# A first feed-forward by seven block products, and a new order of its passes

## The chip, the cores and the metric

One core of a Trainium2 chip runs the kernel in one launch. The metric is the device time of the run in microseconds (us); smaller is better. Five engines work side by side, each through its own queue of instructions in order: TensorE (PE in the profile, with PEld for its weight loads), VectorE (DVE), ScalarE (ACT), GpSimd (POOL) and SyncE (SP, which here only issues transfers). They wait for each other by semaphores.

## The reference

Two decoder layers on x of 512 tokens by 2048 channels, float32. Each layer is a half feed-forward, a mixer, and a half feed-forward; a last norm ends it. What the change touches is the feed-forward:

```
h = h + 0.5 * swiglu(rms_norm(h, g), w_gate, w_up, w_down)
swiglu(x) = (silu(x @ w_gate) * (x @ w_up)) @ w_down
w_gate, w_up: 2048 x 1536     w_down: 1536 x 2048
```

There are four of them: (0,0) at the start, (0,1) and (1,0) between the two mixers, (1,1) at the end. The mixers (dilated attention beside latent attention; pooling beside stick-breaking attention) stay as they are.

## The kernel before

Activations are kept transposed, as 16 blocks of 128 channels by 512 tokens. Every float32 operand of a matmul is split in two: `h`, rounded by ACT to the type that PE takes (line 273 for weights, 312 or 315 for activations), and the rest `l = x - h`, by DVE (lines 274, 313, 316). A product is then three matmuls, h·h, h·l and l·h (`mm3`, lines 302 to 304).

**Weights** come in the order of a plan that is written out ahead (`plan_and_uses`). SP loads blocks of 128 x 512 into 9 `raw` buffers; `split_to` splits each into one of 7 pairs of split buffers, up to 6 blocks ahead of the block in use (`ahead`, line 284). So ACT and DVE always work on splits that PE needs some products later, and their instructions stand in their queues in the order in which the Python code emits them.

**The plain feed-forward** (`ffn`, line 473) is used for (0,0) alone: 12 gate and 12 up products over 16 blocks of channels, then 16 down products over 12 blocks. Its first 16 steps (tiles `gu`) work on two output blocks beside the loading and splitting of x; squares for the norm are summed by POOL (line 395).

**The feed-forward by products** (`ffn_products`, line 595) is used for the other three. Tokens, channels and the pair gate and up are cut in halves, and seven products of sums of blocks stand for eight (the Strassen-Winograd scheme). `Pieces` makes the sums of activations: `early` (line 559) four subtractions (line 563) and two splits per pair of channel blocks, `late` (line 575) the other three operands. The sums of weights are made in place by DVE (line 278) behind the split that used the block last. Hidden channels go in three units of 512. Per unit a pass of three products (tiles `pa`, 144 matmuls: 8 blocks k, 3 products, 2 halves of 128 tokens, 3 matmuls) and a pass of four (tiles `pb`, 192 matmuls). The four-pass needs four weight splits and four sums a k from DVE. In the order of the code: three, four of unit 0, three, four of unit 1, three, four of unit 2.

Behind each four-pass `to_hidden` (line 621) combines the results: eight additions (line 622), four Silus (lines 626, 629), four multiplications with the norm's factor (line 636), and 16 transposes on PE (line 644) per unit, whose output is split into the `hid` blocks that the down products read. It is a generator in the queue `side`; each `tick()` takes its next step. Ticks stand behind each product of the next pass of three, and behind down products for the last unit. The transposes are in PE's queue at the place where the step was emitted, and all that is emitted later waits behind them.

**Down products** (tiles `pd`): 16 output blocks; the first four (`FIRST`) run in two parts, so that units 0 and 1 can be used before unit 2 is ready. The residual comes back from DRAM (`reload`), the result goes to a sink that scales, squares and stores it.

Of the kernel before, what the change touches and what calls it, by code (L numbers as in the profile page):

```python
# [16 lines left out]
P = 128  # L17
S = 512
DM = 2048
# [35 lines left out]

FIRST = 4
# [13 lines left out]
def plan_and_uses():  # L70
# [15 lines left out]
    def ffn_products(i, j, down):  # L86


        for u in range(FF // UNIT):
            c0, c1 = u * UNIT, (u + 1) * UNIT  # L90
            block = lambda name, k: cols(name, i, j, k, k + 1, c0, c1)
            for k in range(HK):
                block("ffn_w_up", k)
                block("ffn_w_up", HK + k)
                block("ffn_w_gate", HK + k)
            for k in range(HK):
                r = len(plan)
                a22, a21, a11, a12 = r, r + 1, r + 2, r + 3
                block("ffn_w_gate", HK + k)
                block("ffn_w_gate", k)  # L100
                block("ffn_w_up", k)
                block("ffn_w_up", HK + k)
                sums[r - 3] = (a22, a21, 1, a22)
                sums[r - 2] = (a21, a11, -1, a21)
                sums[r - 1] = (a11, a22, -1, a11)
                sums[r] = (a12, a12, -1, a11)
        for n in range(0, len(down)):
            d = down[n][0]
            if n % FIRST == 0 and n < FIRST:
                for k0, k1 in ((0, 8), (8, NF)):  # L110
                    for e in down[:FIRST]:
                        cols("ffn_w_down", i, j, k0, k1, e[0] * P, e[0] * P + P)
            elif n >= FIRST:
                cols("ffn_w_down", i, j, 0, NF, d * P, d * P + P)

    def ffn(i, j, first=False):
        f = 0
        if first:
            for k0 in range(0, NK, 4):
                for ff in range(2):  # L120
                    for name in ("ffn_w_gate", "ffn_w_up"):
                        cols(name, i, j, k0, k0 + 4, ff * P, ff * P + P)
            f = 2
        for f in range(f, NF):
            for name in ("ffn_w_gate", "ffn_w_up"):
                cols(name, i, j, 0, NK, f * P, f * P + P)
        for d in range(NK):
            cols("ffn_w_down", i, j, 0, NF, d * P, d * P + P)

    ffn(0, 0, first=True)  # L130
# [86 lines left out]
def trunk(ctx: ExitStack, tc: tile.TileContext, xT, pos_row, pos_col, wts, gains, consts, bias_a_in, bias_b_in, outT):  # L217
# [131 lines left out]
    def load_x(d0, d1):  # L349
        for d in range(d0, d1):  # L350
            xs[d] = blk(f"x{d}")
            nc.sync.dma_start(xs[d], xT[d * P:(d + 1) * P, :])

    nc.scalar.dma_start(gn, gains)
    load_x(0, 4)
    load_to(2)
    load_x(4, 8)
# [78 lines left out]
    def rope_tables():  # L436
# [4 lines left out]
        for _ in range(10):  # L441
            yield
# [29 lines left out]

    def ffn(xg, norm, resid_in, sink, first=False, beside=None):
        hid = {}
        ng = norm.stages() if norm is not None else None

        def half_of(ps, name, n=HK):
            for k, wh, wl in take(name, n):
                mm3(ps, wh, wl, xg[k][0], xg[k][1], k == 0, k == NK - 1)

        def gate(ps):
            t = blk("gate")
            nc.vector.tensor_tensor(t, ps, norm.R, op=ALU.mult)
            nc.scalar.activation(t, t, AF.Silu)
            return t

        def up(f, ps, t):
            u = blk("up")
            nc.vector.tensor_tensor(u, ps, norm.R, op=ALU.mult)
            nc.vector.tensor_tensor(t, t, u, op=ALU.mult)  # L490
            hid[f] = split(t, "hid")

        f0 = 0
        if first:
            pss = [bank("gu") for _ in range(4)]
            for i in range(NK):
                half_of(pss[i % 4], ("ffn_w_gate", "ffn_w_up")[i % 2], 4)
                beside(i)
            f0 = 2
        for f in range(f0, NF):  # L500
            pg, pu = bank("pg"), bank("pu")
            half_of(pg, "ffn_w_gate")
            tick()
            if first and f == 2:
                next(ng)
            half_of(pg, "ffn_w_gate")
            if f == 0:
                next(ng)
            tick()
            half_of(pu, "ffn_w_up")  # L510
            if f == f0:
                finish(ng)
            if first and f == 2:
                up(0, pss[1], gate(pss[0]))
            t = gate(pg)
            tick()
            half_of(pu, "ffn_w_up")
            up(f, pu, t)
            if first and f == 2:
                e = gate(pss[2])  # L520
            elif first and f == 3:
                up(1, pss[3], e)
            tick()
        for job in DOWN:
            pd = bank("pd")
            for n in (8, 4):
                down_half(pd, job, hid, n)
                tick()
            down_done(pd, job, resid_in, sink)
# [65 lines left out]
    def ffn_products(pieces, norm, resid_in, sink, down):  # L595
# [25 lines left out]
        def to_hidden(u, c11, u2, s4, s5, s7, c12):  # L621
            add = lambda o, a, b: nc.vector.tensor_tensor(o, a, b, op=ALU.add)
            for a in both:
                add(s7[a], s7[a], u2[a])
                add(s4[a], s4[a], s7[a])
                nc.scalar.activation(s4[a], s4[a], AF.Silu, scale=norm.r[:, a:a + 1])
                yield
                add(s7[a], s7[a], s5[a])
                nc.scalar.activation(s7[a], s7[a], AF.Silu, scale=norm.r[:, 2 + a:3 + a])
                add(c12[a], c12[a], s5[a])  # L630
                yield
            u2.clear()
            s5.clear()
            for a in both:
                for o, g, r in ((c11, s4, a), (c12, s7, 2 + a)):
                    nc.vector.scalar_tensor_tensor(o[a], o[a], norm.r[:, r:r + 1], g[a], op0=ALU.mult, op1=ALU.mult)
                yield
            s4.clear()
            s7.clear()
            rows = c11 + c12  # L640
# [7 lines left out]
        for u in range(FF // UNIT):  # L648
            p1, p2, p4 = ([bank("pa") for _ in both] for _ in range(3))
            last = HK - 1  # L650
            for k in range(HK):
                product("ffn_w_up", "B11", p1, k, u)
                if k == last:
                    s1 = copied(p1)
                if u == 0:
                    for e in range(k + 1, min(k + 4, HK)):
                        pieces.get(e, "B11", False)
                else:
                    tick()
                product("ffn_w_up", "B21", p2, k, u)  # L660
                if k == last:
                    c11 = added(p2, s1)
                if u == 0:
                    next(late, None)
                else:
                    tick()
                product("ffn_w_gate", "T4", p4, k, u)
                if k == last:
                    s4 = copied(p4)
                if u:  # L670
                    tick()
                elif k > HK // 2:
                    next(ng, None)
            if u == 0:
                finish(ng)
                finish(late)
            del p1, p2, p4
            p5, p7, p6, p3 = ([bank("pb") for _ in both] for _ in range(4))
            for k in range(HK):
                product("ffn_w_gate", "T1", p5, k, u)  # L680
                if k == last:
                    s5 = copied(p5)
# [3 lines left out]
                if k == last:  # L686
                    s7 = copied(p7)
                if k % 2:
                    tick()
                product("ffn_w_up", "T2", p6, k, u)  # L690
                if k == last:
                    u2 = added(p6, s1, s1)
# [3 lines left out]
                if k % 2:  # L696
                    tick()
            side.append(to_hidden(u, c11, u2, s4, s5, s7, added(p3, u2)))
            del p5, p7, p6, p3, s1, c11, u2, s4, s5, s7
        pds = [bank("pd") for _ in range(FIRST)]  # L700
        for pd, job in zip(pds, down):
            for n in (4, 4):
                down_half(pd, job, hid, n)
                tick(2)
        while side:
            tick()
# [226 lines left out]
    norm = Norm(DM)  # L933
    xg = {}
    split_to(0)

    def split_x(d):
        xg[d] = split(xs[d], "xg", scale=g_norm(0)(d))

    def beside(i):  # L940
        if i in (0, 3):
            load_x(8 if i == 0 else 12, 12 if i == 0 else 16)
        if i + 4 < NK:
            split_x(i + 4)
        norm.add(xs[i])

    for d in range(4):
        split_x(d)
    u_diag, u_all = ur[:, 0:P], ur[:, P:2 * P]
    norm1, xg1 = Norm(DM), {}  # L950
    spill0 = dram_x("spill0")

    def started(i):
        beside(i)
        if i == NK - 1:
            nc.scalar.activation(ur, cs[:, 2 * P:4 * P], AF.Copy)

    side.append(rope_tables())
    ffn(xg, norm, lambda d: xs[d], make_sink(g_norm(1), norm1, xg1, spill0), first=True, beside=started)
    xs.clear()  # L960
# [262 lines left out]
```

## Time and profile before

| | us |
|---|---|
| median of 3 runs (2327.45 to 2329.95) | 2327.6 |
| the profiled execution | 2328.22 |
| its span, first to last instruction | 2326.4 |
| PE busy in it | 2249.4 |
| DVE busy | 1450.0 |
| ACT busy | 1051.5 |
| POOL busy | 185.7 |

Matmuls are pipelined: one lasts 0.39 us in the profile, but the next starts 0.23 us after it, so the time of a stretch is the number of its matmuls by the time from start to start, plus what PE waits. The mean granted TensorE clock of the execution was 0.984 of full speed. A row of a window table covers a stretch from A to B in us from the span's start; the count in brackets is that of the instructions that touch it.

### The profile page before, as it was taken

Reading aid. Unit: us, or ns where it says so; the run is one execution under the profiler, and the core shown is the slowest. Engines: PE = TensorE matmul, PEld = TensorE weight load, DVE = VectorE, ACT = ScalarE, POOL = GpSimd, SP = SyncE. Lnnn points to the kernel's source line nnn. Section 1 sums busy time; section 2 is a strip of 40 time slices with the busy share of each in tenths; the row PEclk is TensorE's granted clock in tenths of the full one; section 3 lists DMA queues with packets and bytes.
Section 4 is the critical chain, followed back from the end, with each engine's and each line's share of the span. In section 5 each row is a group of like instructions: output and inputs, shape, how many; then the busy total and the mean of one; then the engine's idle time right before and its main releaser. Section 6 shows DMA issues by size and latency. Waiting matters only on the chain.

```text
span 2326.4 us, 30133 instructions
## 1 busy us (share of the span) xinstructions
PE 2249.4 (97%) x10364; PEld 1882.2 (81%) x10364; DVE 1450.0 (62%) x2460; ACT 1051.5 (45%) x1875; POOL 185.7 (8%) x191
## 2 busy tenths in 40 slices
PE   8999999999999999889999898999999999898997
PEld 6888888989888888778788787788888888687787
DVE  5453344464645688878557787755345679788634
ACT  5332333333334575445446454433235576454443
POOL 3000011000001011000011000011200011000013
PEclk9999999999999999999999999999999999999999
DMA  6333343423224486556676565554332486565544
GB/s 219 100 87 105 104 127 114 122 64 104 74 73 124 134 250 185 166 153 185 179 192 182 165 189 152 156 181 151 98 96 69 127 238 200 154 181 164 148 140 142
DMA packets 193290, 336.94 MB, mean 145 GB/s; under 512 B 21488, under 2 KB 44400, under 8 KB 193136
## 3 DMA queue, kind: packets, MB, share of 16 engines
q1 hardware_dynamic: 163184, 280.89, 40.9%
q10 hardware_dynamic: 23904, 43.11, 5.7%
q0 software_dynamic: 6048, 11.01, 2.9%
q8 instruction: 81, 1.33, 0.2%
q14 instruction: 73, 0.60, 0.1%
HBM read 298.75 MB, written 25.17 MB: 139 GB/s over the span
## 4 chain that ended last, share of the span: by engine, by line
PE 87%; DVE 5%; issue 3%; ACT 2%; DMA 2%; POOL 0%; DVEq 0%; ACTq 0%; POOLq 0%
PE pd L303 7%; PE pd L304 7%; PE pd L302 7%; PE pb L302 5%; PE pb L304 5%; PE pb L303 5%; PE pj L302 4%; PE pj L304 4%; PE pj L303 4%; PE pa L302 3%; PE pa L303 3%; PE pa L304 3%; PE wo L302 3%; PE wo L304 3%; PE wo L303 3%
## 5 line engine op out<-in xcount | busy, mean ns | idle before, releaser
L274 DVE TENSOR_TENSOR wl<-raw,wh 128x512 fp32r<-128x512 f32 (+3 forms) x1087 | 737.2, 688 | 605.1 <-ACT wh L273 569.2
L273 ACT ACTIVATE wh<-raw 128x512 fp32r<-128x512 f32 (+3 forms) x1087 | 652.5, 609 | 749.5 <-DVE wl L274 126.3
L302 PE MATMUL pd<-hidh,wh 128*128 128x512 f32 (+1 forms) x816 | 307.9, 377 | 0.0
L304 PE MATMUL pd<-hidh,wl 128*128 128x512 f32 (+1 forms) x816 | 307.3, 377 | 0.0
L303 PE MATMUL pd<-hidl,wh 128*128 128x512 f32 (+1 forms) x816 | 307.3, 377 | 0.0
L278 DVE TENSOR_TENSOR raw<-raw,raw 128x512 f32<-128x512 f32 x288 | 196.6, 683 | 0.0
L302 PE MATMUL pj<-xgh,wh 128*128 128x512 f32 x464 | 181.7, 392 | 0.0
L304 PE MATMUL pj<-xgh,wl 128*128 128x512 f32 x464 | 180.8, 390 | 0.0
L303 PE MATMUL pj<-xgl,wh 128*128 128x512 f32 x464 | 180.7, 389 | 0.0
L302 PEld LDWEIGHTS pd<-hidh,wh 128*128 128x128 f32 x816 | 153.6, 188 | 28.1
L303 PEld LDWEIGHTS pd<-hidl,wh 128*128 128x128 f32 x816 | 153.6, 188 | 28.0
L304 PEld LDWEIGHTS pd<-hidh,wl 128*128 128x128 f32 x816 | 153.6, 188 | 27.8
L302 PE MATMUL pa<-wh,pbh 128*128 128x512 f32 x432 | 175.1, 405 | 0.0
L395 POOL TENSOR_TENSOR sq<-sq,sq 128x512 f32<-128x512 f32 (+1 forms) x65 | 81.5, 1253 | 1155.8 <-ACT sq L387 1155.8
L303 PE MATMUL pa<-wl,pbh 128*128 128x512 f32 x432 | 171.6, 397 | 0.0
L304 PE MATMUL pa<-wh,pbl 128*128 128x512 f32 x432 | 171.3, 397 | 0.0
L302 PE MATMUL pb<-wh,pth 128*128 128x512 f32 x288 | 112.2, 390 | 0.9 <-DVE s L618 0.9
L304 PE MATMUL pb<-wh,ptl 128*128 128x512 f32 x288 | 112.0, 389 | 0.0
L303 PE MATMUL pb<-wl,pth 128*128 128x512 f32 x288 | 112.0, 389 | 0.0
L304 PEld LDWEIGHTS pj<-xgh,wl 128*128 128x128 f32 x464 | 87.1, 188 | 18.2
L303 PEld LDWEIGHTS pj<-xgl,wh 128*128 128x128 f32 x464 | 87.2, 188 | 17.4
L302 PEld LDWEIGHTS pj<-xgh,wh 128*128 128x128 f32 x464 | 87.2, 188 | 17.3
(265 smaller groups left out, 3941.6 us busy)
## 6 DMA issues: line engine op xcount, KB each, us to landing
raw<-wts SPq DMA_DIRECT2D x940, 256.0 KB, 2.8
spill<-x ACTq DMA_DIRECT2D x80, 256.0 KB, 3.0
x<-spill ACTq DMA_DIRECT2D x80, 256.0 KB, 3.1
raw<-wts SPq DMA_DIRECT2D x83, 192.0 KB, 2.4
sq<-sq POOLq DMA_DIRECT2D x42, 256.0 KB, 4.9
raw<-wts SPq DMA_DIRECT2D x48, 128.0 KB, 2.4
x<-xT SPq DMA_DIRECT2D x16, 256.0 KB, 5.0
outT<-sc SPq DMA_DIRECT2D x16, 256.0 KB, 2.3
```

The costliest lines, as they stand in the source:

```text
L273: nc.scalar.activation(h, src, AF.Copy)
L274: nc.vector.tensor_tensor(low, src, f32(h), op=ALU.subtract)
L278: nc.vector.tensor_tensor(to, a, b, op=ALU.add if sign > 0 else ALU.subtract)
L302: nc.tensor.matmul(out, ah, bh, start=start, stop=False)
L303: nc.tensor.matmul(out, ah, bl, start=False, stop=False)
L304: nc.tensor.matmul(out, al, bh, start=False, stop=stop)
L395: nc.gpsimd.tensor_tensor(acc, acc, sq, op=ALU.add)
```

## The change

- Feed-forward (0,0) goes through `ffn_products` too, with its own generator `first_pieces` that makes the pieces from x beside the first pass; the plain `ffn` is gone. x is loaded in pairs between the first weight blocks; squares are summed by transfers that add (`by_dma`) and the residual is read again from `xT`.
- `PASSES` sets the order of the passes for all four: three of unit 0, three of 1, four of 0, three of 2, four of 1, four of 2. The late pieces and the norm move from the first pass into the second. Results of a pass of three are kept (`part`) until its four.
- `to_hidden` has a second `yield` behind each step of additions; a pass of four has 8 ticks instead of 16.
- The first four down products run in three parts, one per unit; `rope_tables` joins `side` only behind the second.

```diff
+PASSES = ((0, 0), (1, 0), (0, 1), (2, 0), (1, 1), (2, 1))
...
-        for u in range(FF // UNIT):
+        for u, four in PASSES:
...
-                for k0, k1 in ((0, 8), (8, NF)):
+                for k0, k1 in ((0, 4), (4, 8), (8, NF)):
...
-    ffn(0, 0, first=True)
+    ffn_products(0, 0, PAIR_DOWN)
...
-    def load_x(d0, d1):
-        for d in range(d0, d1):
+    nc.scalar.dma_start(gn, gains)
+    for k in range(HK):
+        for d in (k, HK + k):
             xs[d] = blk(f"x{d}")
             nc.sync.dma_start(xs[d], xT[d * P:(d + 1) * P, :])
-
-    nc.scalar.dma_start(gn, gains)
-    load_x(0, 4)
-    load_to(2)
-    load_x(4, 8)
+        load_to(min(3 * k + 2, NRAW - 1))
...
-        for _ in range(10):
+        for _ in range(4):
             yield
...
                 nc.scalar.activation(s4[a], s4[a], AF.Silu, scale=norm.r[:, a:a + 1])
                 yield
+                yield
                 add(s7[a], s7[a], s5[a])
                 nc.scalar.activation(s7[a], s7[a], AF.Silu, scale=norm.r[:, 2 + a:3 + a])
                 add(c12[a], c12[a], s5[a])
+                yield
                 yield
...
                     nc.vector.scalar_tensor_tensor(o[a], o[a], norm.r[:, r:r + 1], g[a], op0=ALU.mult, op1=ALU.mult)
                 yield
+                yield
             s4.clear()
             s7.clear()
+            yield
...
+        def ahead_pieces():
+            for k in range(HK):
+                for e in range(k + 1, min(k + 4, HK)):
+                    pieces.get(e, "B11", False)
+                yield
+                yield
+                yield
+
+        def then_late():
+            for _ in range(HK):
+                next(late, None)
+                yield
+                yield
+            yield from ng
...
+        def four(u):
             p5, p7, p6, p3 = ([bank("pb") for _ in both] for _ in range(4))
+            q = part.pop(u)
...
+            q["c12"] = added(p3, q["u2"])
+            turned[u] = to_hidden(u, **q)
+            side.append(turned[u])
+
+        feed = ahead_pieces() if feed is None else feed
+        rest = then_late()
+        for u, is_four in PASSES:
+            if is_four:
+                four(u)
+            elif u == 0:
+                three(u, lambda: next(feed, None))
+                finish(feed)
+            elif u == 1:
+                three(u, lambda: next(rest, None))
+                finish(rest)
+            else:
+                three(u, tick)
+                finish(turned[0])
         pds = [bank("pd") for _ in range(FIRST)]
-        for pd, job in zip(pds, down):
-            for n in (4, 4):
-                down_half(pd, job, hid, n)
+        for u in range(2):
+            finish(turned[u])
+            for pd, job in zip(pds, down):
+                down_half(pd, job, hid, UNIT // P)
                 tick(2)
-        while side:
-            tick()
+        side.extend(beside)
+        finish(turned[2])
...
+    norm0, in0 = Norm(DM, bc=False, sums=2, by_dma=True), Pieces(0)
...
+    def first_pieces():
+        for k in range(HK):
+            bs = []
+            for d in (k, HK + k):
+                b = blk("xb")
+                nc.scalar.activation(b, xs[d], AF.Copy, scale=g_norm(0)(d))
+                bs.append(b)
+            in0.add(k, *bs)
+            del bs, b
+            next(in0.work[k])
+            yield
+            finish(in0.work[k])
+            yield
+            for d in (k, HK + k):
+                norm0.add(xs.pop(d))
+            yield
+        nc.scalar.activation(ur, cs[:, 2 * P:4 * P], AF.Copy)
+
+    feed = first_pieces()
+    split_to(0)
+    for _ in range(5):
+        next(feed)
+    ffn_products(in0, norm0, reload([xT[d * P:(d + 1) * P, :] for d in range(NK)], PAIRS),
+                 make_sink(g_norm(1), norm1, xg1, spill0), PAIR_DOWN, feed, [rope_tables()])
```

In `three(u, beside)`, `beside()` stands behind each of the 24 products of the pass; the products themselves are as before.

## Rows read from the trace of the kernel before

**Rows 1.** The page's part 1: busy us, share of the span, instructions.
```profile
PE 2249.4 (97%) x10364; PEld 1882.2 (81%) x10364; DVE 1450.0 (62%) x2460; ACT 1051.5 (45%) x1875; POOL 185.7 (8%) x191
```

**Rows 2.** Windows by stage: stretch, length, busy by engine, granted clock, DMA share, GB/s.
```profile
0.00:57.03 57.03, 48.72 (x192) 38.93 (x193) 29.71 (x42) 33.49 (x57) 19.80 (x19) 0.97 0.65 219
...
276.05:406.61 130.56, 130.56 (x578) 108.11 (x576) 63.19 (x80) 47.16 (x79) 18.13 (x14) 1.00 0.38 121
...
841.51:1233.31 391.80, 373.10 (x1650) 306.84 (x1648) 283.43 (x466) 196.26 (x333) 20.52 (x16) 0.97 0.64 179
1233.31:1622.65 389.34, 372.38 (x1650) 306.47 (x1648) 281.68 (x431) 186.15 (x315) 27.57 (x17) 0.98 0.58 169
1915.81:2314.39 398.58, 378.00 (x1812) 316.86 (x1810) 274.21 (x442) 196.96 (x348) 33.70 (x26) 0.97 0.56 162
```

**Rows 3.** The list of waits of PE: us in total, times, longest.
```profile
PE ht L644 <- DVE s L636: 53.4, 21, 7.3
```

**Rows 4.** Windows by pass of feed-forward (1,0): three, four, three, first down products.
```profile
1311.31:1355.73 44.42, 36.96 (x161) 29.70 (x160) 33.03 (x53) 20.89 (x35) 0.00 (x0) 0.92 0.51 143
1355.73:1399.25 43.52, 43.52 (x193) 36.05 (x192) 37.34 (x60) 22.81 (x38) 0.00 (x0) 1.00 0.68 194
1399.25:1444.03 44.78, 37.37 (x162) 30.12 (x160) 33.12 (x53) 21.02 (x35) 0.00 (x0) 0.89 0.50 142
...
1487.55:1505.58 18.03, 15.94 (x78) 12.77 (x76) 14.74 (x24) 6.86 (x12) 0.00 (x0) 1.00 0.40 100
```

**Rows 5.** The chain that ended last: start, length, what.
```profile
1115.61 0.87 PE ht L644 x8
1257.95 1.68 PE nps L402 x16
```

**Rows 6.** Timeline of DVE, second three-pass of (1,0): start, length, instruction, idle before.
```profile
1314.28 1.41 DVE L622 TENSOR_TENSOR s<-s,s 128x512 f32<-128x512 f32 x2
...
1317.67 1.29 DVE L622 TENSOR_TENSOR s<-s,s 128x512 f32<-128x512 f32 x2
...
1320.28 1.41 DVE L622 TENSOR_TENSOR s<-s,s 128x512 f32<-128x512 f32 x2
...
1328.13 1.41 DVE L636 SCALAR_TENSOR_TENSOR s<-s,r,s 128x512 f32<-128x512 f32 x2
```

**Rows 7.** Timeline of ACT in the same stretch.
```profile
1315.79 0.72 ACT L626 ACTIVATE s<-s,r 128x512 f32<-128x512 f32 x1 [3.64 <-DVE s L622]
1316.41 0.62 ACT L273 ACTIVATE wh<-raw 128x512 fp32r<-128x512 f32 x1
```

**Rows 8.** Timeline of PE in the same stretch: the first transpose.
```profile
1327.01 0.48 PE L644 MATMUL ht<-cs,s 128*128 128x128 f32 x1 [6.01 <-DVE s L636]
```

**Rows 9.** Timeline of DVE in a pass of four.
```profile
1275.23 0.68 DVE L274 TENSOR_TENSOR wl<-raw,wh 128x512 fp32r<-128x512 f32 x1
1275.83 0.69 DVE L278 TENSOR_TENSOR raw<-raw,raw 128x512 f32<-128x512 f32 x1
```

**Rows 10.** Timeline of PE at the start.
```profile
5.90 0.79 PE L302 MATMUL gu<-xgh,wh 128*128 128x512 f32 x1 [5.90 <-ACT xgh L315]
...
24.90 0.50 PE L303 MATMUL gu<-xgl,wh 128*128 128x512 f32 x1 [2.41 <-DVE xgl L316]
```

**Rows 11.** Windows of 4 us at the start.
```profile
8.00:12.00 4.00, 4.00 (x11) 3.22 (x11) 2.34 (x4) 1.55 (x3) 0.00 (x0) 1.00 1.06 400
...
24.00:28.00 4.00, 3.10 (x8) 2.46 (x9) 3.46 (x5) 1.76 (x3) 0.96 (x2) 0.67 0.76 255
```

**Rows 12.** Timeline of ACT at the start.
```profile
18.23 0.71 ACT L315 ACTIVATE xgh<-x,gn 128x512 fp32r<-128x512 f32 x1
...
19.88 0.71 ACT L315 ACTIVATE xgh<-x,gn 128x512 fp32r<-128x512 f32 x1
```

**Rows 13.** Timeline of DVE while a piece is made.
```profile
801.76 0.42 DVE L563 TENSOR_TENSOR t<-xb 128x256 f32<-128x256 f32 x1
...
803.23 0.68 DVE L899 TENSOR_TENSOR x<-wo,x 128x512 f32<-128x512 f32 x1
```

More of the change, by code (lines that the diff above doesn't have):

```diff
@@ L86, in ffn_products @@
     def ffn_products(i, j, down):
-        for u in range(FF // UNIT):
+        for u, four in PASSES:
             c0, c1 = u * UNIT, (u + 1) * UNIT
             block = lambda name, k: cols(name, i, j, k, k + 1, c0, c1)
-            for k in range(HK):
+            for k in range(HK if not four else 0):
                 block("ffn_w_up", k)
@@ L95, in ffn_products @@
                 block("ffn_w_gate", HK + k)
-            for k in range(HK):
+            for k in range(HK if four else 0):
                 r = len(plan)
@@ L114, in ffn_products @@
                 cols("ffn_w_down", i, j, 0, NF, d * P, d * P + P)
[L116 to L128, printed above, removed]
-    ffn(0, 0, first=True)
+    ffn_products(0, 0, PAIR_DOWN)
     for half in range(2):
@@ L470, in rope_tables @@
         rope_b["cos"], rope_b["sin"] = cb, sb
[L473 to L502, printed above, removed]
-            tick()
[L504 to L526, printed above, removed]
-                down_half(pd, job, hid, n)
-                tick()
-            down_done(pd, job, resid_in, sink)
     def down_half(pd, job, hid, n):
@@ L593, in get, with ffn_products @@
             return self.of[k].pop(name) if last else self.of[k][name]
-    def ffn_products(pieces, norm, resid_in, sink, down):
+    def ffn_products(pieces, norm, resid_in, sink, down, feed=None, beside=()):
         hid = {}
@@ L646, in to_hidden, with three @@
                 hid[u * (UNIT // P) + f] = split(pt, "hid")
-        for u in range(FF // UNIT):
+        def ahead_pieces():
[11 more added lines that the diff above has]
+            yield from ng
+        last = HK - 1
+        part, turned = {}, {}
+        def three(u, beside):
             p1, p2, p4 = ([bank("pa") for _ in both] for _ in range(3))
-            last = HK - 1
+            q = part[u] = {}
             for k in range(HK):
@@ L653, in ffn_products @@
                 if k == last:
[L654 to L659, printed above, removed]
+                    q["s1"] = copied(p1)
+                beside()
                 product("ffn_w_up", "B21", p2, k, u)
                 if k == last:
[L662 to L666, printed above, removed]
+                    q["c11"] = added(p2, q["s1"])
+                beside()
                 product("ffn_w_gate", "T4", p4, k, u)
                 if k == last:
[L669 to L677, printed above, removed]
+                    q["s4"] = copied(p4)
+                beside()
+        def four(u):
             p5, p7, p6, p3 = ([bank("pb") for _ in both] for _ in range(4))
+            q = part.pop(u)
+            s1 = q.pop("s1")
             for k in range(HK):
@@ L681, in ffn_products @@
                 if k == last:
-                    s5 = copied(p5)
+                    q["s5"] = copied(p5)
                 if k % 2:
@@ L686, in ffn_products @@
                 if k == last:
-                    s7 = copied(p7)
-                if k % 2:
-                    tick()
+                    q["s7"] = copied(p7)
                 product("ffn_w_up", "T2", p6, k, u)
                 if k == last:
-                    u2 = added(p6, s1, s1)
+                    q["u2"] = added(p6, s1, s1)
                 if k % 2:
@@ L695, in ffn_products @@
                 product("ffn_w_up", "B22", p3, k, u)
[L696 to L699, printed above, removed]
+            q["c12"] = added(p3, q["u2"])
[15 more added lines that the diff above has]
+                finish(turned[0])
         pds = [bank("pd") for _ in range(FIRST)]
-        for pd, job in zip(pds, down):
-            for n in (4, 4):
-                down_half(pd, job, hid, n)
+        for u in range(2):
+            finish(turned[u])
+            for pd, job in zip(pds, down):
+                down_half(pd, job, hid, UNIT // P)
                 tick(2)
-        while side:
-            tick()
+        side.extend(beside)
+        finish(turned[2])
         for pd, job in zip(pds, down):
@@ L930, in pe_rope @@
         nc.gpsimd.tensor_tensor(v, a, b, op=ALU.add)
[L933 to L949, printed above, removed]
+    norm0, in0 = Norm(DM, bc=False, sums=2, by_dma=True), Pieces(0)
     norm1, xg1 = Norm(DM), {}
     spill0 = dram_x("spill0")
[L953 to L960, printed above, removed]
+    u_diag, u_all = ur[:, 0:P], ur[:, P:2 * P]
+    def first_pieces():
[21 more added lines that the diff above has]
+                 make_sink(g_norm(1), norm1, xg1, spill0), PAIR_DOWN, feed, [rope_tables()])
     xg, norm = xg1, norm1
```

## The prediction

> **What bounds the kernel now.** I read the page's busy shares first: PE is busy 97% of 2326.4 us [rows 1], so only fewer matmuls or fewer idle stretches of TensorE can shorten the run. Then one table of windows by stage [rows 2]. The down products of the first feed-forward are the plain case: 576 matmuls in 130.56 us, 0.2267 us from start to start (p below), no idle time. The first feed-forward ends at 406.61 us; its first 57.03 us hold only 192 matmuls, whose pace would be 43.5. The three feed-forwards that are products already take 391.80 and 389.34 us, and the last 398.58 with the output. Their floor is 7 products x 8 k x 2 halves x 3 units x 3 = 1008 matmuls (228.5), 48 transposes at 0.87/8 (5.2), 16 matmuls of the norm (1.68) [rows 5] and the down products (130.56): 366.0. So the first two lose 25.8 and 23.4 us; the last I take at their mean, 24.6, because its passes have the same code. Together 73.8.
>
> Where that lies: the list of waits has one entry of weight for PE, the transposes of line 644 waiting for the products of line 636 on DVE, 53.4 us in 21 waits [rows 3]. The table by pass [rows 4] shows it: a pass of four products takes 43.52 us, exactly 192p, and loses nothing; the pass of three after it takes 44.42 and 44.78 where 144p + 16 transposes are 34.4; the first stretch of down products takes 18.03 where 60p + 16 transposes are 15.3. The granted clock of these three-passes is 0.89 to 0.92: after the long wait part of the matmuls run at the lower level. So 10 + 10 + 3 us a feed-forward.
>
> Why it waits, from the timeline [rows 6 to 8]. The pass of three starts at 1311.31. `to_hidden` emits an addition step at every tick, one per product. A step is two additions on DVE, then Silu on ACT; the next weight split on ACT stands behind that Silu in order, DVE's half of the split behind that, and the next additions behind that. So steps start at 1314.28, 1317.67, 1320.28: 3.4 us after a step of the first kind, 2.6 after the second, while PE goes on 1.36 us (6p) per product. PE reaches the first transposes after 42 matmuls, 9.5 us into the pass, and waits 6.01 us at once; the last product of line 636 starts at 1328.13 and a pair takes 1.41, 18.2 us into the pass.
>
> **The change, part by part.** Durations are of the profiled execution (2328.2 us with what lies around its span; median of the runs 2327.6), and the sum is made against it.
>
> (a) The half pace. Idle yields now stand between the steps, and the transposes come at the 14th tick instead of the 7th. In the third pass of three (the pass after `four(0)`) PE meets them after 14 products, 84p = 19.0 us. On DVE the first step still starts 3.0 us in; between steps there is one more split (0.60 from one DVE instruction to the next [rows 9]), so steps follow at 4.0, 3.2, 4.0, 3.2, and then two pairs of line 636 (1.41 each) with two splits between (1.2): 3.0 + 14.4 + 1.4 + 1.2 + 1.4 = 21.4. PE waits 21.4 - 19.0 = 2.4 us; I take 2.3, since the first three transposes need not wait for the last product. In its place of 10. What the wait leaves behind is late splits: DVE enters `four(1)` some 4 us behind its usual lead, and makes it good there, since a four-pass costs it 32 x 1.2 = 38.6 of 43.5 us.
>
> (b) The order three, three, four, three, four, four. The second pass of three has no `to_hidden` at all now, only the late pieces and the norm: its wait of 10 us goes. What is late next is `four(2)`, which carries four addition steps of unit 1 in its own eight ticks. DVE there: 25 splits with their sums at 1.2 = 30, the last additions of `four(1)` 1.3, three steps before the last split, each with the turn over ACT, 2.7 + 2.0 + 2.7: 38.7, about 39.7 us into the pass; PE needs that split 31 products in, at 42.2. It holds by 2.5 us. If it did not, PE would wait split by split: rival D. The bound from the other side is a stall of nothing.
>
> (c) The first down products. They run by unit: four products for unit 0, then unit 1's transposes in one burst, four for unit 1, then unit 2's. Unit 1's last two products on DVE end about 11.2 us into the stretch, PE arrives at 48p = 10.9: 0.3. The four splits of the turned block then stand behind one addition step of unit 2 on DVE (1.3) and a weight split that waits for ACT (1.3): PE has its second matmul 1.8 us late. Unit 2: DVE ends 25.8 us in, PE arrives at 25.4; 0.5 with the splits. So 2.1 + 0.5, in place of 3. From both sides: 0 if DVE keeps its lead, and 10, the present wait of a three-pass, if the burst meets a late DVE as it does now.
>
> (a) to (c) leave 2.3 + 2.1 + 0.5 = 4.9 us a feed-forward (bounds 0 and 12). Gains: 25.8, 23.4 and 24.6 less 4.9 each: 59.1.
>
> (d) The first feed-forward as products. Against 1728 matmuls it has 1008 + 576 = 1584, 144p = 32.6 us fewer, and 48 transposes and 8 norm matmuls more (6.0). Weights are cut 72 blocks more often (56 blocks a unit against 32), and 96 sums on DVE come in; both lie beside PE, as in the other three, where the four-pass at 43.52 shows them covered. If that cover went, DVE's 38.6 us a pass would still not set the end.
>
> Its first pass is another matter. x has to be loaded, scaled, subtracted and split beside the matmuls. By DMA: 16 blocks of x and 24 of weights in the pass, 10.5 MB; at the 400 GB/s that the start shows [rows 11] 26 us: no bound. By ACT, per k two scaled copies, two splits, two squares, three weight splits: nine instructions. Three of the same kinds take 19.88 - 18.23 = 1.65 us [rows 12], so 4.95; and the piece's splits wait for four subtractions on DVE, 803.23 - 801.76 = 1.47 us [rows 13], of which a weight split covers half: 5.7 us a k, where PE needs 18p = 4.1. ACT sets this pass. Its order: PE's first matmul now starts at 5.90 [rows 10]; here a second block of x, a second scaled copy and the subtractions come first, some 3 us more: 9. But ACT then has the first squares and the whole second piece (5 us, to 14) and six weight splits at 0.55 in its queue before anything else, and PE's second product needs the first of those: PE really starts at 15. The splits end at 17.3; the third piece takes ACT one more turn of 5.7, so PE reaches k = 2 at 23.0. Five more turns to k = 7 (51.5) and its own 4.1 end the pass at 55.6. Bounds: 51 (ACT at 4.95 without the wait) and 77 (rival C). I take 55.6; the present start, same number of blocks of x, ends at 57.03.
>
> After it: two passes of three 65.3, norm 1.7, three of four 130.6, transposes 5.2, down products 130.6, waits 4.9: ends at 393.9 against 406.61. Gain 12.7. `rope_tables` moves from the gate products into the last twelve down products: 24 ticks for some 14 steps, DVE busy there under half of the time [rows 2]; nothing. The residual is read again from xT on ACT's queue, three blocks ahead, as the other stages do; nothing, unless those loads come late, and then the wait would stand at line 539.
>
> (e) Down weights in three parts rather than two: the same blocks in another order; nothing.
>
> Sum: 59.1 + 12.7 = 71.8; 2328.2 - 71.8 = 2256.4, less 0.6 for the median: **2256 us**.
>
> **Rivals.**
> B, the half pace spreads the waits without removing them. For it: the chain DVE, ACT, ACT, DVE of [rows 6, 7] is untouched, and at 4.0 and 3.2 us for two products it is slower than PE (2.7). Against: 7 more products of room. Price: 12 us left a feed-forward, 7.1 more in each of four: 2284.
> C, the first pass at the lower clock. For it: after the idle 2.41 us at 24.90 [rows 10] the stretch 24 to 28 was granted 0.67, part of it at 1.2 GHz [rows 11]; ACT will make PE wait about 1.6 us at every k. Against: idle 1.6 is shorter than 2.41. Price: a k costs 36p = 8.2 us instead of 5.7, so the pass ends near 77: 2277. The Trainium skill, "TensorE: Matmul & The Clock Gate", section "HAM oscillation — how this bites in real kernels", speaks for this rival: where each tile's compute is short against the wait for its operand, the array is throttled again at every tile. By that rule the time would be this rival's; the trace agrees with it for the one wait of 2.41 us and shows no run of shorter ones.
> D, slower: the two passes of four in a row exhaust DVE's lead. Seven split buffers are 9.5 us of PE, less the block in use and 1.3 us of splitting 6.8. If the lag passes that (I have 4), PE waits at each split in `four(2)`, falls to 1.2 GHz, and the pass takes 384p = 87 instead of 43.5 in all four stages: 2256 + 174 = 2430. Against it: the 2.5 us in hand under (b).
> E, the gain is not there: what leaves the three-passes returns in (c) in full and the first feed-forward pays for its start what the 26.6 us of fewer instructions give: 2328.
>
> **How the numbers follow.** Forecast 0.60, own range 2238 to 2275 (waits of 1 to 9 us a feed-forward, the first pass 51 to 60). B 0.22, C 0.08, D 0.07, E 0.03. The range 2236 to 2290 leaves out D, E, the upper third of B and the thin ends. Within 0.2% (4.7 us, about what cannot be told from no change) only E: 0.03. Faster 0.90, slower 0.07.
>
> **What would show it.** In the table by pass: the second pass of three at about 34.4 us; the third at 36.6; all three of four at 43.5; the first down stretch with 96 matmuls and 32 transposes near 27.9. The waits: line 644 behind 636 under 20 us for four feed-forwards, not 53.4. The first pass of the first feed-forward ending at 51 to 60 us with PE waiting for pieces, not for DMA. Wrong would be: `pb` matmuls that wait for a weight split (D), a granted clock near 0.5 over the first 55 us (C), transposes that wait 5 us or more (B).

## The result, and the profile after

The changed kernel takes 2268.27 us (median of 4 runs, 2267.64 to 2269.59) against 2327.57 (median of 4 runs): ratio 0.9744, 95% interval 0.9727 to 0.976. Forecast were 2256 us and a range of 2236 to 2290. The profiled execution took 2269.59 us with a span of 2267.8, so 58.6 us of span are gone where 71.8 were forecast.

The page's part 1 [rows 1]: PE's share of the span went from 97 to 98%, and DVE has 120 us more to do.

```profile
PE 2218.3 (98%) x10272; PEld 1853.0 (82%) x10272; DVE 1570.6 (69%) x2694; ACT 1111.5 (49%) x2002; POOL 159.0 (7%) x190
```

The table of windows, columns as in [rows 2], first by stage (the feed-forwards (0,0), (0,1), (1,0), (1,1)), then by pass of (0,0) (three, three, four, three, two of four together, first down products), then the third pass of three in the other stages:

```profile
0.00:398.47 398.47, 377.27 (x1649) 306.85 (x1649) 311.63 (x513) 214.22 (x373) 31.99 (x33) 1.00 0.65 192
833.42:1208.66 375.24, 370.35 (x1649) 304.70 (x1648) 281.99 (x466) 194.35 (x333) 14.13 (x16) 1.00 0.66 187
1208.66:1581.38 372.72, 368.49 (x1650) 303.81 (x1648) 279.80 (x431) 184.04 (x315) 21.23 (x17) 1.00 0.60 177
1874.57:2255.83 381.26, 374.50 (x1811) 314.27 (x1809) 272.65 (x442) 194.51 (x348) 27.35 (x26) 1.00 0.58 169
...
0.00:55.62 55.62, 39.55 (x144) 28.95 (x145) 40.48 (x80) 44.46 (x80) 11.60 (x17) 1.00 0.99 298
55.62:90.11 34.49, 34.49 (x162) 28.81 (x160) 29.81 (x54) 24.56 (x48) 2.28 (x2) 1.00 0.77 223
90.11:133.63 43.52, 43.52 (x194) 36.04 (x192) 37.34 (x60) 22.80 (x38) 0.00 (x0) 1.00 0.69 194
133.63:172.99 39.36, 36.88 (x162) 29.66 (x160) 32.22 (x53) 21.53 (x36) 0.00 (x0) 0.96 0.55 161
172.99:260.31 87.32, 87.32 (x386) 72.00 (x384) 81.77 (x132) 43.72 (x74) 0.00 (x0) 1.00 0.65 182
260.31:289.43 29.12, 26.48 (x129) 21.22 (x128) 22.63 (x36) 12.65 (x24) 0.00 (x0) 1.00 0.43 125
...
944.07:983.12 39.05, 36.80 (x161) 29.44 (x160) 32.15 (x53) 21.41 (x36) 0.00 (x0) 0.96 0.56 163
1319.31:1355.84 36.53, 34.98 (x161) 28.54 (x160) 31.78 (x53) 20.25 (x35) 0.00 (x0) 1.00 0.60 174
1985.22:2024.22 39.00, 36.75 (x161) 29.44 (x160) 32.15 (x53) 21.41 (x36) 0.00 (x0) 0.96 0.55 164
```

Beside [rows 2] the four stages are 8.1, 16.6, 16.6 and 17.3 us shorter: 58.6, the whole difference of the spans. The forecast had 12.7, 20.9, 18.5 and 19.7. By pass, against [rows 4]: the second pass of three is at its matmuls' pace (34.49), two passes of four in a row take 87.32 = 2 x 43.66, and the third pass of three takes 36.53 in (1,0), as worked out, but 39.36, 39.05 and 39.00 in the others, at a granted clock of 0.96, which means that part of it ran at the lower of TensorE's two levels (1.2 and 2.4 GHz).

The longest entries of PE's list of waits (total, times, longest), against [rows 3]; line 575 is the old 644:

```profile
PE ht L575 <- DVE s L565: 14.7, 18, 2.2
PE pa L290 <- ACT pbh L300: 13.1, 5, 8.9
PE pd L290 <- ACT hidh L300: 2.9, 4, 0.7
PE pa L290 <- ACT wh L261: 2.9, 1, 2.9
```

The 53.4 us of the transposes are 14.7. Timelines of PE, then of DVE in the third pass of three of (1,0) (against [rows 6]), then of ACT in that of (0,0) (against [rows 7]):

```profile
8.90 0.80 PE L290 MATMUL pa<-wh,pbh 128*128 128x512 f32 x1 [8.90 <-ACT pbh L300]
...
14.70 0.80 PE L290 MATMUL pa<-wh,pbh 128*128 128x512 f32 x1 [2.87 <-ACT wh L261]
...
24.63 0.39 PE L290 MATMUL pa<-wh,pbh 128*128 128x512 f32 x1
...
33.69 0.50 PE L290 MATMUL pa<-wh,pbh 128*128 128x512 f32 x1 [0.74 <-ACT pbh L300]
...
51.11 0.50 PE L290 MATMUL pa<-wh,pbh 128*128 128x512 f32 x1 [1.15 <-ACT pbh L300]
...
272.59 0.44 PE L575 MATMUL ht<-cs,s 128*128 128x128 f32 x2 [1.13 <-DVE s L565]
...
275.61 0.50 PE L290 MATMUL pd<-hidh,wh 128*128 128x512 f32 x1 [0.72 <-ACT hidh L300]
...
1339.95 0.44 PE L575 MATMUL ht<-cs,s 128*128 128x128 f32 x2 [1.33 <-DVE s L565]
```

```profile
1322.28 1.41 DVE L549 TENSOR_TENSOR s<-s,s 128x512 f32<-128x512 f32 x2
1325.06 1.29 DVE L262 TENSOR_TENSOR wl<-raw,wh 128x512 fp32r<-128x512 f32 x2 [1.37 <-ACT wh L261]
1326.27 1.28 DVE L549 TENSOR_TENSOR s<-s,s 128x512 f32<-128x512 f32 x2
...
1329.48 1.41 DVE L549 TENSOR_TENSOR s<-s,s 128x512 f32<-128x512 f32 x2
...
1333.41 1.29 DVE L549 TENSOR_TENSOR s<-s,s 128x512 f32<-128x512 f32 x2
...
1339.15 1.41 DVE L565 SCALAR_TENSOR_TENSOR s<-s,r,s 128x512 f32<-128x512 f32 x2
```

```profile
138.08 1.28 ACT L553 ACT_TABLE_LOAD   x1 [3.62 <-DVE s L549]
139.38 0.72 ACT L553 ACTIVATE s<-s,r 128x512 f32<-128x512 f32 x1
```

In (1,0) the steps start 4.0, 3.2 and 3.9 us after one another, the last pair of products ends at 1340.56, 21.25 us into the pass, and PE waits 1.33 us. In (0,0) the first Silu has a load of 1.28 us ahead of it (ACT_TABLE_LOAD, by which ACT changes its table of functions). In (0,0) no Silu has run before it; in (0,1) and (1,1), which have such a load too, functions of the mixers with loads of their own came in between. The load stands in the chain DVE, ACT, ACT, DVE, so what follows in that chain comes later: PE reaches the first transposes 0.36 us later than in (1,0) and then waits 2.20 us in place of 1.33.

### The profile page after: what moved, and what is told of

The parts are those of the page before. It is cut to its first block, busy times and chain, and to the rows that moved or that the text cites. A ratio compares the mean times of both kernels' runs of the same rounds, so it can differ in the third digit from the quotient of the medians.

```text
span 2267.8 us, 30596 instructions
## 1 busy us (share of the span) xinstructions
PE 2218.3 (98%) x10272; PEld 1853.0 (82%) x10272; DVE 1570.6 (69%) x2694; ACT 1111.5 (49%) x2002; POOL 159.0 (7%) x190
## 4 chain that ended last, share of the span: by engine, by line
PE 92%; DVE 3%; ACT 1%; issue 1%; DMA 0%; POOL 0%; DVEq 0%; ACTq 0%; POOLq 0%
PE pb L291 8%; PE pb L290 8%; PE pb L292 8%; PE pd L291 7%; PE pd L292 7%; PE pd L290 7%; PE pa L290 5%; PE pa L292 5%; PE pa L291 5%; PE pj L290 5%; PE pj L292 5%; PE pj L291 5%; PE wo L290 3%; PE wo L292 3%; PE wo L291 3%; PE pr L290 2%
## 5 line engine op out<-in xcount | busy, mean ns | idle before, releaser
L262 DVE TENSOR_TENSOR wl<-raw,wh 128x512 fp32r<-128x512 f32 (+3 forms) x1159 | 780.3, 686 | 465.2 <-ACT wh L261 442.4
L266 DVE TENSOR_TENSOR raw<-raw,raw 128x512 f32<-128x512 f32 x384 | 262.4, 683 | 0.0
L290 PE MATMUL pa<-wh,pbh 128*128 128x512 f32 x576 | 230.0, 399 | 16.0 <-ACT pbh L300 13.1
L291 PE MATMUL pa<-wl,pbh 128*128 128x512 f32 x576 | 227.6, 395 | 0.3
L292 PE MATMUL pa<-wh,pbl 128*128 128x512 f32 x576 | 227.5, 395 | 0.0
L292 PE MATMUL pb<-wh,ptl 128*128 128x512 f32 x384 | 149.4, 389 | 0.0
L291 PE MATMUL pb<-wl,pth 128*128 128x512 f32 x384 | 149.4, 389 | 0.0
L290 PEld LDWEIGHTS pa<-wh,pbh 128*128 128x128 f32 x576 | 110.2, 191 | 40.2 <-ACT pbh L300 14.8
L292 PEld LDWEIGHTS pa<-wh,pbl 128*128 128x128 f32 x576 | 109.8, 191 | 25.0 <-DVE pbl L301 1.9
L291 PEld LDWEIGHTS pa<-wl,pbh 128*128 128x128 f32 x576 | 109.9, 191 | 24.1 <-DVE wl L262 2.0
```

The lines of the kernel that those rows point to most:

```text
L262: nc.vector.tensor_tensor(low, src, f32(h), op=ALU.subtract)
L266: nc.vector.tensor_tensor(to, a, b, op=ALU.add if sign > 0 else ALU.subtract)
L290: nc.tensor.matmul(out, ah, bh, start=start, stop=False)
L291: nc.tensor.matmul(out, ah, bl, start=False, stop=False)
L292: nc.tensor.matmul(out, al, bh, start=False, stop=stop)
```

## The experiments

Ratios are to the kernel before, run on the same chip (2328.5 to 2329.4 us). "After" is the changed kernel.

### The pace alone

The kernel before with nothing but the idle yields:

```diff
                 nc.scalar.activation(s4[a], s4[a], AF.Silu, scale=norm.r[:, a:a + 1])
                 yield
+                yield
...
                 add(c12[a], c12[a], s5[a])
+                yield
                 yield
...
                 yield
+                yield
             s4.clear()
             s7.clear()
+            yield
```

> The kernel before with nothing but the idle yields in to_hidden (the half pace); old order, plain first feed-forward. Theory P (the additions' chain over VectorE and ScalarE against the tick at which the transposes stand in TensorE's queue): the second and third pass of three of each feed-forward by products fall from 44.4 to 46.4 us to 36.4 to 39.4, the first down stretch loses its 2.7 us of waiting; about 18 us a stage, 2273 us in all. Rival O (the order of the passes does it, the pace only spreads the wait): under a third of that comes, 2310 us or more.

Measured: 2273.29 us, ratio 0.976 (0.9747 to 0.9774), as expected: 55 of the 59 us. Its windows: a pass of three of (1,0), the one with a table load in (0,1):

```profile
1294.22:1330.73 36.51, 34.96 (x161) 28.53 (x160) 31.77 (x53) 20.24 (x35) 0.00 (x0) 1.00 0.56 173
920.97:960.36 39.39, 36.91 (x162) 29.68 (x160) 32.13 (x53) 21.25 (x36) 0.00 (x0) 0.96 0.52 161
```

So the pace brings a waiting pass of three to 36.5 us (39.4 with a table load) in the old order too, and both such passes of a stage gain. The order isn't needed for it.

### The pace of unit 0 taken back

After, with `if u:` ahead of each new yield, so that unit 0's steps come at every product again.

> The changed kernel with the additions of unit 0 alone back at full pace (those that run in the third pass of three); units 1 and 2 and the order stay. Theory P: that pass goes from 36.4 to 39.4 us back to 44.5 to 46.5 in all four stages, about 7 us each, 2296 us. Rival O: the pass of three without additions ahead of it gives VectorE the room, the time stays at 2268 us.

Measured: 2299.29 us, ratio 0.9873 (0.986 to 0.9886), where 2296 was expected. The window of the third pass of three of (0,0), and the wait:

```profile
133.43:179.99 46.56, 37.82 (x162) 30.41 (x160) 33.11 (x53) 22.29 (x36) 0.00 (x0) 0.89 0.45 137
```

```profile
PE ht L579 <- DVE s L567: 40.1, 20, 7.3
```

31 us come back in four passes, and the granted clock of 0.89 is again that of [rows 4].

### The old order, at half the pace

The three later feed-forwards in the order three, four, three, four, three, four, the late pieces and the norm in the first pass again (by a generator of their own, which is not shown here):

```diff
+OLD = ((0, 0), (0, 1), (1, 0), (1, 1), (2, 0), (2, 1))
...
-        for u, four in PASSES:
+        for u, four in (PASSES if (i, j) == (0, 0) else OLD):
...
```

> The changed kernel with the later three feed-forwards in the old order three, four, three, four, three, four at the half pace; the first stays in the new order. Theory P: both later passes of three wait as the one of the new order does (4.5 us where ScalarE loads its Silu table, 2.0 where it has it), but the burst of unit 1's transposes in the down products goes, worth 2.7: 2261 us, slightly faster. Rival O: the order is what took the waits away, 8 us a stage come back, 2292 us.

Measured: 2264.63 us, ratio 0.9724 (0.9711 to 0.9737), where 2261 was expected. Feed-forward (1,0) and its first stretch of down products (96 matmuls, 16 transposes):

```profile
1205.55:1576.00 370.45, 367.41 (x1650) 303.76 (x1649) 279.14 (x431) 184.57 (x315) 27.56 (x17) 1.00 0.59 178
1443.57:1467.05 23.48, 23.48 (x113) 19.58 (x112) 15.96 (x26) 8.58 (x15) 0.00 (x0) 1.00 0.37 113
```

The new order is no gain at this pace. The old one has two passes of three that wait, 36.5 where 34.4 is their pace, so its second one loses some 2.1 us; but its first down products don't wait at all: 23.48 is 96p and 16 transposes. The new order has one pass that waits and a late burst of transposes among the down products: 29.12 where 96p and 32 transposes are 25.2, a loss of 3.9. So the three later stages are 1.2 to 2.3 us shorter in the old order (370.45 against 372.72 for (1,0)).

The run of the pace alone has the plain first feed-forward, and its later three stages agree with those of this run within 0.3 us. So the difference of the medians, 8.7 us, is about what the products are worth in the first feed-forward. Part by part, then, the pace brought about 55 us, the products 9, and the order took some 4 back.

### The table loaded early

After, with one Silu of a few values at the start of the first pass of four, where ACT has time:

```diff
+            if u == 0:
+                nc.scalar.activation(small("tb"), norm.r, AF.Silu)
```

> The changed kernel with one Silu of four columns on ScalarE at the start of the first pass of four, its result unused, so that the table of 1.28 us is loaded there and not in the chain of additions. Theory T (the load is in the chain and its 1.3 us also drop TensorE's clock): the third pass of three of the first, second and fourth feed-forward falls from 39.4 to 36.4 us as in the third, 2260 us. Rival: something else than the table sets those stages apart, 2268 us.

Measured: 2261.11 us, ratio 0.9709 (0.9696 to 0.9723). The third pass of three of (0,0):

```profile
133.48:169.92 36.44, 34.94 (x161) 28.53 (x160) 31.76 (x53) 20.24 (x35) 0.00 (x0) 1.00 0.56 174
```

All four stages now have 36.4 to 36.5, at a clock of 1.00. The load of 1.28 us cost 2.5 to 2.9 us a pass: 0.36 ahead of the transposes, 0.9 as their wait (2.20 in place of 1.33), and the rest as matmuls behind it at the lower clock, 0.43 us from start to start in place of 0.23.

### Silu one tick behind its additions

After, with the idle `yield` ahead of each Silu instead of behind it, so that ACT's weight splits stand ahead of a Silu that would wait for DVE. The last addition of a step now stands ahead of that `yield`, so DVE's own order stays as it was and only the Silus move:

```diff
                 add(s4[a], s4[a], s7[a])
+                yield
                 nc.scalar.activation(s4[a], s4[a], AF.Silu, scale=norm.r[:, a:a + 1])
                 yield
-                yield
                 add(s7[a], s7[a], s5[a])
+                add(c12[a], c12[a], s5[a])
+                yield
                 nc.scalar.activation(s7[a], s7[a], AF.Silu, scale=norm.r[:, 2 + a:3 + a])
-                add(c12[a], c12[a], s5[a])
-                yield
                 yield
```

> The changed kernel with each Silu one tick behind its additions, in the yield that was idle (and the last addition of the step ahead of that Silu), so that no weight split on ScalarE stands behind a Silu that waits for VectorE. Theory P says that the turn VectorE, ScalarE, ScalarE, VectorE sets the step (4.0 and 3.2 us); without it a step costs VectorE 2.5 us, under two products of TensorE (2.7), the additions end about 18 us into the third pass of three, ahead of the transposes at 19.0, and that pass is 34.6 us in all four stages, its table load included; the bursts in the down products lose about 1 us each: 2250 us. Rival V (VectorE's plain amount of work sets the end): no change, 2268 us.

Measured: 2240.18 us, ratio 0.9619 (0.9606 to 0.9633), 10 us better than expected. Windows: third pass of three of (0,0) and of (1,0), the whole of (1,0), first down products of (0,0); then what is left of the wait; then DVE's last pair of products in the third pass of three of (1,0):

```profile
133.56:168.94 35.38, 34.95 (x161) 28.53 (x160) 31.77 (x53) 21.75 (x36) 0.00 (x0) 1.00 0.61 179
1303.51:1338.05 34.54, 34.54 (x162) 28.60 (x160) 32.05 (x53) 20.49 (x35) 0.00 (x0) 1.00 0.60 184
1192.86:1559.53 366.67, 366.67 (x1650) 304.05 (x1648) 279.94 (x431) 185.85 (x315) 21.21 (x17) 1.00 0.60 180
...
255.98:281.38 25.40, 25.40 (x130) 21.33 (x128) 20.72 (x34) 10.72 (x19) 0.00 (x0) 1.00 0.37 110
```

```profile
PE ht L575 <- DVE s L565: 1.3, 6, 0.2
```

```profile
1320.94 1.41 DVE L565 SCALAR_TENSOR_TENSOR s<-s,r,s 128x512 f32<-128x512 f32 x2
```

The turn over the two engines was the cause of nearly all of the transposes' wait (14.7 us became 1.3), those of the down products too: 29.12 became 25.40, where the expectation had taken off 1 us only. The turn is shorter and not gone: the steps now start 3.4 and 2.6 us after one another, where 2.5 was expected, and the last pair of products ends 18.84 us into the pass, only 0.2 us before PE comes to the transposes at 19.04. What is left of the wait stands in the three stages with a table load. Feed-forward (1,0) takes 366.67 us, within 0.7 of the floor of 366.0, with PE busy all the time.

### The squares of x in the second pass

To shorten ACT's turn in the first pass, the squares of x go from `first_pieces` to the second pass of three, where the norm's matmuls then come five products later:

```diff
-            for d in (k, HK + k):
-                norm0.add(xs.pop(d))
...
+                if xs:
+                    norm.add(xs.pop(n // 2 + n % 2 * HK))
...
```

> The changed kernel with the 16 squares of x for the first norm on ScalarE in the second pass of three instead of the first. Theory A (ScalarE's nine instructions a k set the first pass): seven instructions, 1.04 us a k less, the pass ends at about 49 us instead of 55.6, 2262 us. Rival D (loads of x and weights set it): unchanged, 2268 us.

Measured: 2281.22 us, ratio 0.9796 (0.9782 to 0.9809): a miss. The windows of the first and the second pass, and PE's timeline of the norm:

```profile
0.00:50.75 50.75, 38.84 (x145) 28.20 (x146) 39.84 (x81) 37.40 (x66) 0.20 (x4) 0.97 0.78 271
50.75:104.24 53.49, 41.00 (x162) 32.44 (x160) 32.95 (x56) 31.56 (x62) 13.60 (x15) 0.81 0.83 202
```

```profile
92.14 0.59 PE L387 MATMUL nps<-ones,sq 128*128 128x1 f32 x2 [6.24 <-DMA sq<-sq]
96.14 3.15 PE L387 MATMUL nps<-ones,sq 128*128 128x1 f32 x14 [3.41 <-DMA sq<-sq]
```

The first pass did become shorter, 50.75 for 55.62: without two squares ACT's turn was mostly 4.77 us in place of 5.81. (The adding transfers left the pass with the squares; their share in the gain was not tested apart.) But the second lost 19 us. The squares are added up by transfers, seven in a row for each of two sums, the last issued at 90.12; PE's norm waited for them twice, 9.7 us together, and the pass ran at a granted clock of 0.81.

### Both, and with eight sums

The two edits above together, then that with `sums=8` in place of 2, which leaves one addition to each sum.

> The changed kernel with both: each Silu one tick behind its additions, and the squares of x in the second pass. If both theories hold the gains add, since they lie in different passes: 2243 us. If the squares in the second pass delay the splits ahead of the first pass of four, the gain of the first feed-forward is smaller: 2250 us.

> The kernel of e7_both with eight sums of squares for the first norm instead of two, so that each takes one adding transfer and none waits for another. Theory S (in e7 the norm's matmuls waited 7.4 and 2.3 us for the last of a chain of seven adding transfers a sum): those waits go, the second pass of three is about 37 us with 32 norm matmuls instead of 16, the first pass ends at 50.3 as in e7, and the time is 2237 us. Rival: the ten squares and splits a pass on ScalarE are late as such, the pass of three stays above 40 us, 2243 us or more.

Measured: 2253.85 us, ratio 0.9677 (0.9663 to 0.969), and 2251.09, ratio 0.9667 (0.9654 to 0.968). Both are misses: the first is 4 us above the higher of its two expected values, the second 14 us above its own, and they are 14 and 11 us slower than Silu apart alone. The second pass with eight sums, and its norm:

```profile
50.47:100.34 49.87, 46.66 (x209) 39.64 (x208) 33.19 (x56) 31.59 (x62) 8.45 (x9) 0.87 0.73 186
```

```profile
82.70 1.62 PE L387 MATMUL nps<-ones,sq 128*128 128x1 f32 x14
85.77 9.44 PE L387 MATMUL nps<-ones,sq 128*128 128x1 f32 x50 [1.45 <-DMA sq<-sq]
```

The chain of additions is gone and most of the wait with it (1.45 us are left), but the norm now has 64 instructions on PE in place of 16 (the expectation counted 32), and they ran in 11.1 us. The second pass stayed above 40 us, as the rival said, but the norm takes most of that, not late splits on ACT. Either way the second pass pays back more than the 4.9 us won in the first.

### The old order with Silu apart, and the best version

The old order of the later three with Silu apart; then after with Silu apart and the table loaded early.

> The kernel of e3 (later three feed-forwards in the old order, half pace) with each Silu one tick behind its additions. Theory P (once the turn over ScalarE is gone no pass waits, in whatever order): the same as e5_silu_apart within 0.2%, 2240 us. Rival O (two passes of three in a row, or the additions in the third one alone, are still worth something): 2250 us or more.

> The kernel of e5_silu_apart with the early Silu of e4 besides. In e5 the third pass of three is still 35.4 us in the stages that load the table and 34.5 in the one that does not. Theory T: all four are at 34.5, 3 x 0.85 us less than e5, 2237.5 us. Rival: with the Silus apart the table load is covered already and the 0.85 us have another cause, 2240 us.

Measured: 2241.06 us, ratio 0.9626 (0.9613 to 0.9639): as Silu apart in the new order (2240.18), so without the waits the order is worth nothing either way. The last: **2237.65 us, ratio 0.9608 (0.9595 to 0.9621)**, as expected, and the fastest of all. Its list of waits has no entry for the transposes any more. Its third pass of three and first down products of (0,0):

```profile
133.56:168.10 34.54, 34.54 (x162) 28.62 (x161) 32.13 (x53) 20.51 (x35) 0.00 (x0) 1.00 0.62 184
...
255.14:280.54 25.40, 25.40 (x128) 21.31 (x128) 20.72 (x34) 10.68 (x19) 0.00 (x0) 1.00 0.35 110
```

## Why the prediction was right, and where not

**The mechanism of the pace was right**, and it carries nearly all of the gain; the part given to the order was not (b). The long wait of the transposes lay in the turn between the two engines; half the pace gives that turn more products of room. It does so alone (2273.29), and taking it back for one unit loses 31 us again.

**(a) The third pass of three**: 36.53 us in (1,0) against 36.6, the pairs' end 21.25 us in against 21.4. In the other three stages the term was too small by 2.4 to 2.8 us, 7.6 in all. The prediction took its chain from (1,0), where no table load stands; in (0,1) and (1,1) the trace of before had one in the same place, which the prediction left out. ACT in (0,1), before:

```profile
924.70 1.28 ACT L626 ACT_TABLE_LOAD   x1 [3.62 <-DVE s L622]
```

The Trainium skill, "ScalarE activation tables: per-element evaluation and per-set limits", section "What a function is on this engine", puts functions of different sets one load of 1283 ns apart and those of one set none. The trace agrees on the load: three on the line of the first Silu, 1283 ns each. In (1,0), where only copies and squares lie between its Silus and those of (0,1), it shows none. The group in the list of lines of after (busy, mean ns, idle before):

```profile
L553 ACT ACT_TABLE_LOAD x3 | 3.8, 1283 | 10.9 <-DVE s L549 10.9
```

**(b) The order.** Two fours in a row hold: 87.32 us, no split late; rival D is refuted. But the prediction gave the 10 us of the second pass of three to the order. The two runs of the old order show that half the pace alone brings that pass to 36.5 us, 8 of the 10, and takes the wait of the first down products away besides (23.48 us, no wait), where the new order keeps one of 3.9. So at this pace the order cost 1.2 to 2.3 us a stage.

**(c) The first down products**: 29.12 against 27.9, four times 1.2 us. The price of unit 1's burst was too small: PE waits 1.13 us for the products where 0.3 were forecast, and from the first of the 16 transposes to the next down product it takes 4.42 us, where the same work without waits takes 1.7 (with Silu apart the whole stretch is 3.7 us shorter).

**The term that was mis-sized** is the waits left in a feed-forward: 4.9 us in the prediction, 6.7 in (1,0) and 9.2 in (0,1) measured (372.72 and 375.24 less 366.0). 7.6 in (a) and 4.9 in (c) are 12.5 of the 13.2 us that were missed; the floor itself was 0.7 too low (366.67 in a stage without waits), which the last stage, taken at a mean, made good in part. Rival B, with 12 a feed-forward and 2284, was 16 us off on the other side.

**(d) The first feed-forward**: its first pass ended at 55.62 us against 55.6, the steady turn was 5.81 against 5.7. That it came out within 0.02 us is luck: ACT split the piece of k = 2 at 21.38 us, where the forecast had PE at 23.0, each turn took 0.1 more, and the last k took 4.5 in place of 4.1. PE itself came to k = 2 only at 24.63, because matmuls up to 20.45 us started 0.43 us apart, and so waited first at k = 4, 33.69; that cost nothing, since ACT set the end. ACT's first split of a piece, one turn:

```profile
38.82 1.15 ACT L300 ACTIVATE pbh<-xb 128x512 fp32r<-128x512 f32 x2 [0.83 <-DVE xb L490]
```

In a turn of 5.81 us ACT is busy for 4.98 and waits 0.83 for DVE's subtractions, so the turn is full without the loads of x, although the DMA share of this pass is 0.99. Rival C is refuted: behind the four waits of 0.74 to 1.16 us matmuls started 0.23 us apart again within a few. The Trainium skill, "TensorE: Matmul & The Clock Gate", section "HAM oscillation — how this bites in real kernels", speaks of compute that is short against the wait for its operand. That is not the case of this pass, where a k's 4.1 us stand against a wait of 1.16, and the trace shows no throttling behind these waits. The stage gained 8.1 us instead of 12.7, by (a), (c) and the floor.

**Rival E** is refuted by the result itself.

## What to carry to other kernels

Where two engines hand a chain to one another in program order, look first at what else stands in their queues between the hand-overs: moving one instruction behind work that doesn't wait (each Silu one tick later) was worth 28 us more, where the reordering of whole passes was worth nothing. A duration taken from one stage holds for the others only if the rows there are the same: look for a table load, or another clock, in each. And a sum that is built up by transfers needs its chain counted to the end before its start is moved back.

## What was not expected of the hardware

- One load of 1.28 us on ACT made PE's wait 2.20 us in place of 1.33, and the pass of three fell to a granted clock of 0.96: 2.5 to 2.9 us lost for 0.9 of wait there.
- Copies and squares between two stages' Silus needed no load: there is none in (1,0), where only such lie between.
- At the very start matmuls were 0.43 us apart until 20.45 us, as they are in stretches at the lower level, while the windows gave a granted clock of 1.00 there. The trace's first record of the clock is of 20.53 us, so the column says nothing of the time before.
- A transfer that adds to a block took 5.0 us from issue to landing (the page, median of 56), so a sum of seven in a row needs some 35 us (an estimate, 7 x 5.0).
